# Ten gate projections of a hybrid decoder step, computed in pairs with seven block products instead of eight

## The chip, the cores and the metric

The kernel runs on one core of a Trainium2 chip. A core has five engines that run side by side and wait for one another through semaphores: TensorE (PE, matrix products; its weight loads are listed as PEld), VectorE (DVE), ScalarE (ACT), GpSimd (POOL) and SyncE (SP, which issues most DMAs). The metric is the device time of one execution in microseconds; each kernel is executed several times and the median is taken. One further execution is recorded by the hardware profiler, and all rows of the trace come from that one.

## The reference

One layer of a decoder on 512 prompt tokens and 8 sample tokens (T = 520 columns), model width 1024, all in float32:

```python
h = _rmsnorm(x, norm1_g[l]) * (1.0 + sc1) + sh1
u = h @ w_in[l]                                   # 1024 x 8192
qa, fa, ia, oga, xb, yb, ga, gb = _split_cols(u)  # eight parts of 1024 columns
... o_a = HGRN2 recurrence of qa, fa, ia, oga;  o_b = RG-LRU recurrence of xb, yb ...
merged = sigmoid(ga) * (o_a @ w_branch_a[l]) + sigmoid(gb) * (o_b @ w_branch_b[l])
x = x + g1 * (merged @ w_out[l])
h2 = _rmsnorm(x, norm2_g[l]) * (1.0 + sc2) + sh2
x = x + g2 * (square(relu(h2 @ w_ff1[l])) @ w_ff2[l])
y = _rmsnorm(x, final_norm_g)
```

The change concerns the two gate parts of `u`, `ga` and `gb`: 16 output tiles of 128 columns, each a product of a 1024 x 128 block of `w_in` with `h`.

## The kernel before, in words

Activations lie transposed: 128 features on the partitions, the 520 tokens along the free axis, in two halves of 260 (`HALF`). Every float32 operand of a large product is split into a high part (a cast to fp32r, on ACT) and a low part (the difference, on DVE). A product is then three fp32r products, high x high, high x low and low x high, summed in PSUM (`products`, L151). An output tile takes 8 blocks of the inner dimension x 3 x 2 halves = 48 products of 128 x 128 by 128 x 260 (`gemm`).

A weight tile (1024 x 128, 512 KB) is loaded by SP into one of four staging buffers (`wst`), split into `whi` and `wlo` (`_split_w`, ACT at L112, DVE at L115), and used. There are two places for split tiles in the pool `whl`; `split_place` takes them in turn (place `2 * (nsplit % 2)`), and the split of tile n + 2 is asked for when tile n is taken (`AHEAD = 2`), so it can start when the products of tile n are done.

The stages, in order: a start phase; eight HGRN2 heads taken two at a time, with the RG-LRU tiles between them; the 16 gate tiles, first eight of `gb`, then eight of `ga`; the 16 branch products (`branch` for b, `merge` for a); eight tiles of `w_out`; then the MLP, whose second product already uses seven block products for eight (`_split_pair`, `product`). The tail of the last two heads (`head_prompt` for head 6, then for head 7, then `heads_sample_done`) is a chain of small steps between PE, ACT and DVE that runs beside the gate tiles. Before the change `end_recurrences` and `begin_tail` follow gate tile b6; `begin_tail` closes the memory pools of the recurrences and calls `load_branches`, in which POOL loads the recurrences' outputs from DRAM (L885 for `o_b`, L889 for `o_a`) and ACT and DVE split them. Each gate tile is evicted by one sigmoid on ACT straight from PSUM (L175). Between the tiles lie sixteen modulation steps (`mod`, L397): each loads two row blocks of `w_mod` into `wst` and multiplies them with 16 small products into the bank `pt`.

PSUM has eight banks: two double ones (`pmm`), two of `pps`, one `ppt`, one `ppb`. The order of each engine's instructions is fixed when the program is built, by a list scheduler that follows program order as priority; `urgent()` raises an eviction's priority.

Of the kernel before, what the change touches and what calls it, by code (L numbers as in the profile page):

```python
# [35 lines left out]
ROWS = "rows"  # L36

# [6 lines left out]
BUFS = {"e": 4, "g": 6, "xb": 2, "xc": 2, "xcs": 2, "gate": 4, "ag": 2, "hs": 3, "y": 3, "ma": 8, "rs": 1, "sq": 1, "t": 5, "sqs": 2,  # L44
# [32 lines left out]
class Kernel:  # L77
# [55 lines left out]
    def ready_w(self, tile, loads=LOADS):  # L133
        while self.wnext_split < len(self.worder) and self.worder[self.wnext_split][0] <= tile:
            while self.wnext_load < min(self.wnext_split + loads, len(self.worder)):
                i = self.worder[self.wnext_load][1]
                self.wstage[i] = self._load_w(self.wspecs[i], self.wst)
                self.wnext_load += 1
            i = self.worder[self.wnext_split][1]
            st = self.wstage.pop(i)  # L140
            self.wsplit[i] = st.rearrange("p k n -> p (k n)") if ROWS in self.wspecs[i] else self._split_w(st, self.split_place())
# [52 lines left out]
    def slot(self, pool, tag, dt=F32):  # L194
        return pool.tile([128, T], dt, tag=tag, name=tag, bufs=BUFS.get(tag))

# [341 lines left out]
    def head(self, h, first=None):  # L538
# [29 lines left out]
        for j, t in enumerate((f, X[:, 1], q)):  # L568
            nc.vector.tensor_copy(fkq[:, j, :NB], t[:, L:])
# [9 lines left out]
        for b in range(NB):  # L579
            nc.scalar.activation(st[:, b], st[:, b], AF.Copy, scale=fkq[:, 0, b:b + 1])  # L580
# [17 lines left out]
    def head_sample_state(self, h, after):  # L598
        nc = self.nc
        *_, vb, st, fkq = self.opened[h]  # L600
        for b in range(NB):
            ins = nc.vector.scalar_tensor_tensor(st[:, b], vb[:, b], fkq[:, 1, b:b + 1], st[:, b], OP.mult, OP.add)
# [3 lines left out]
    def heads_sample(self, hs):  # L606
        nc = self.nc
        po = self.pps.tile([128, 512], F32, name="ps")
        for e, h in enumerate(hs):
            *_, st, fkq = self.opened[h]  # L610
            for b in range(NB):
                j, c = 32 * (b % 4), 256 * e + 128 * (b // 4)
                nc.tensor.matmul(po[j:j + 32, c:c + 128], fkq[:, 2], st[:, b], start=True, stop=True)
        return po

    def heads_sample_done(self, hs, po):
        nc = self.nc
        ev = self.hg.tile([128, 512], F32, name="sev", bufs=1)
# [7 lines left out]
    def heads_prompt(self, hs):  # L626
# [82 lines left out]
    def head_prompt(self, h, tb, at):  # L709
# [4 lines left out]
        pk = self.ppt.tile([128, 512], F32, name="pt")  # L714
# [4 lines left out]
        pkv = self.ppt.tile([128, 512], F32, name="pt")  # L719
# [10 lines left out]
        po = self.ppt.tile([128, 512], F32, name="pt")  # L730
        for c in range(NC):
            s = slice(c * C, (c + 1) * C)
            nc.tensor.matmul(po[:, s], at[:, c], vn[:, s], start=True, stop=c == 0)
            if c:
                nc.tensor.matmul(po[:, s], Q[:, s], S[:, (c - 1) * 128:c * 128], start=False, stop=True)
        o = self.slot(self.hg, "g")
        ss = self.sm.tile([128, 16], F32, name="ss")
        for c in range(NC):
            s = slice(c * C, (c + 1) * C)
            nc.scalar.activation(o[:, s], po[:, s], AF.Square, accum_out=ss[:, c:c + 1])  # L740
        nc.vector.tensor_scalar(ss[:, :NC], ss[:, :NC], 1.0 / 128, EPS, OP.mult, OP.add)
# [4 lines left out]
        pt = self.ppt.tile([128, 512], F32, name="pt")  # L746
# [1159 lines left out]
```

## Time and profile before

| | before |
|---|---|
| median of three runs | 1019.62 us (1018.96 to 1022.07) |
| the profiled execution | 1015.0 us, of which the recorded span is 1013.2 us |
| granted TensorE clock, mean | 0.995 |
| PE busy | 992.3 us, 98% of the span |
| PEld busy | 964.7 us, 95% |
| DVE busy | 673.8 us, 67% |
| ACT busy | 512.2 us, 51% |
| POOL busy | 130.4 us, 13% |
| sigmoid of the first of the eight `gb` tiles, last of them, last of the eight `ga` tiles | 396.6, 438.9 and 494.6 us |
| first product step of a branch tile a evicted | 553.3 us |

In the rows that follow, a group or an instruction names its line of the kernel, its engine, its operation and the tiles it writes and reads (`mm<-h,whi`: into PSUM tile `mm` from `h` and `whi`); then the partitions x elements of its output and input. A row of the timeline begins with the start and the duration in microseconds, `x4` means four alike merged into one row, and brackets hold the idle time before it and what ended it. A row of windows gives a stretch of the span, its length, and the busy time with the number of instructions for each engine.

### The profile page before, as it was taken

Reading aid. Unit: us, or ns where it says so; the run is one execution under the profiler, and the core shown is the slowest. Engines: PE = TensorE matmul, PEld = TensorE weight load, DVE = VectorE, ACT = ScalarE, POOL = GpSimd, SP = SyncE. Lnnn points to the kernel's source line nnn. Section 1 sums busy time; section 2 is a strip of 40 time slices with the busy share of each in tenths; the row PEclk is TensorE's granted clock in tenths of the full one; section 3 lists DMA queues with packets and bytes.
Section 4 is the critical chain, followed back from the end, with each engine's and each line's share of the span. In section 5 each row is a group of like instructions: output and inputs, shape, how many; then the busy total and the mean of one; then the engine's idle time right before and its main releaser. Section 6 shows DMA issues by size and latency. Waiting matters only on the chain. (4 is left out here: it accounts for less than half of the span.)

```text
span 1013.2 us, 23554 instructions
## 1 busy us (share of the span) xinstructions
PE 992.3 (98%) x9738; PEld 964.7 (95%) x9738; DVE 673.8 (67%) x1417; ACT 512.2 (51%) x963; POOL 130.4 (13%) x253
## 2 busy tenths in 40 slices
PE   6999999999999999999999999999999999999997
PEld 5899999999989999999999999999999999999996
DVE  7686867695785867346233448777767776777685
ACT  6364745735654573345111224466555645646663
POOL 4320000000000010002000000022321331232050
PEclk9999999999999999999999999999999999999998
DMA  9974354344344444339756787322672483273242
GB/s 298 314 214 119 97 164 127 103 122 135 107 137 116 124 147 127 95 98 304 205 167 177 231 245 207 102 86 50 151 176 64 98 196 104 53 175 86 63 84 85
DMA packets 205373, 145.80 MB, mean 144 GB/s; under 512 B 6742, under 2 KB 193774, under 8 KB 205258
## 3 DMA queue, kind: packets, MB, share of 16 engines
q1 hardware_dynamic: 194034, 128.08, 43.1%
q0 software_dynamic: 11216, 16.18, 7.4%
q8 instruction: 76, 1.25, 0.5%
q14 instruction: 31, 0.25, 0.1%
q10 hardware_dynamic: 16, 0.03, 0.0%
HBM read 123.61 MB, written 13.39 MB: 135 GB/s over the span
## 5 line engine op out<-in xcount | busy, mean ns | idle before, releaser
L151 PE MATMUL mm<-h,whi 128*128 128x260 f32 (+1 forms) x2944 | 488.5, 285 | 0.0
L151 PEld LDWEIGHTS mm<-h,whi 128*128 128x128 f32 x2944 | 409.2, 188 | 2.9 <-issue 1.4
L151 PE MATMUL mm<-h,wlo 128*128 128x260 f32 x1472 | 302.4, 285 | 0.0
L115 DVE TENSOR_TENSOR wlo<-wst,whi 128x1024 fp32r<-128x1024 f32 x164 | 200.0, 1221 | 133.5 <-ACT whi L112 132.2
L112 ACT CAST whi<-wst 128x1024 fp32r<-128x1024 f32 x164 | 171.7, 1049 | 213.6 <-PE mm L151 166.2
L151 PEld LDWEIGHTS mm<-h,wlo 128*128 128x128 f32 x1472 | 229.5, 188 | 0.9 <-issue 0.6
L151 PE MATMUL mm<-a,whi 128*128 128x260 f32 x512 | 83.0, 284 | 0.0
L151 PEld LDWEIGHTS mm<-a,whi 128*128 128x128 f32 x512 | 70.0, 188 | 2.1 <-ACT whi L112 1.6
L885 POOL DMA_DIRECT2D t<-obT_d x8 | 4.3, 541 | 396.9 <-PE pb L790 300.1
L151 PE MATMUL mm<-a,wlo 128*128 128x260 f32 x256 | 51.4, 282 | 0.0
L1262 DVE TENSOR_TENSOR f<-f 128x260 f32<-128x260 f32 x64 | 27.3, 426 | 27.8 <-ACT f L1257 27.2
L1254 POOL TENSOR_TENSOR ft<-ft,fsh 128x8 f32<-128x8 f32 x28 | 18.4, 658 | 206.6 <-DVE ft L1248 206.6
L1251 ACT ACTIVATE ft<-ft,fsh 128x512 f32<-128x512 f32 (+2 forms) x36 | 24.0, 675 | 36.0 <-DVE ft L1248 36.0
L151 PE MATMUL mm<-b,whi 128*128 128x260 f32 x256 | 41.7, 285 | 0.0
L151 PEld LDWEIGHTS mm<-a,wlo 128*128 128x128 f32 x256 | 39.4, 188 | 0.0
L151 PEld LDWEIGHTS mm<-b,whi 128*128 128x128 f32 x256 | 35.0, 188 | 2.1 <-ACT whi L112 2.1
L672 DVE TENSOR_TENSOR X<-X,tb 128x512 f32<-128x512 f32 x48 | 30.9, 684 | 5.4 <-PE ps L660 4.2
L1296 POOL DMA_DIRECT2D ma<-snap x28 | 26.5, 960 | 40.1 <-issue 32.3
L1278 POOL DMA_DIRECT2D ma<-snap x28 | 26.4, 943 | 38.0 <-DMA ma<-snap 22.7
L1257 ACT ACTIVATE f<-ft 128x520 f32<-128x520 f32 (+1 forms) x36 | 20.8, 587 | 15.0 <-POOL ft L1255 13.0
L580 ACT ACTIVATE st<-st,fkq 128x128 f32<-128x128 f32 x64 | 19.8, 395 | 14.1 <-DMA st<-in_state_hgrn_dram 12.4
L151 PE MATMUL mm<-b,wlo 128*128 128x260 f32 x128 | 25.6, 282 | 0.0
(576 smaller groups left out, 1865.5 us busy)
## 6 DMA issues: line engine op xcount, KB each, us to landing
wst<-in_w_in_dram SPq DMA_DIRECT2D x64, 512.0 KB, 4.1
wst<-in_w_mod_dram SPq DMA_DIRECT2D x32, 512.0 KB, 3.8
wst<-in_w_ff_dram SPq DMA_DIRECT2D x64, 256.0 KB, 3.6
wst<-in_w_ff_dram SPq DMA_DIRECT2D x32, 512.0 KB, 4.7
wm<-in_w_mod_dram SPq DMA_DIRECT2D x8, 1024.0 KB, 10.8
st<-in_state_hgrn_dram SPq DMA_DIRECT2D x8, 512.0 KB, 6.7
vb<-vd SPq DMA_DIRECT2D x8, 512.0 KB, 3.7
out_dram<-st SPq DMA_DIRECT2D x8, 512.0 KB, 3.9
```

Of the source, the lines that this page charges most:

```text
L112: ins = self.nc.scalar.copy(hi, st)
L115: self.nc.vector.tensor_tensor(lo, st, hi.bitcast(F32), OP.subtract)
L151: self.last_product = self.nc.tensor.matmul(ps[s][:, :c.stop - c.start], x, y[:, c], start=first and n == 0, stop=last and n == 2)
L580: nc.scalar.activation(st[:, b], st[:, b], AF.Copy, scale=fkq[:, 0, b:b + 1])
L672: last = nc.vector.tensor_tensor(half, half, factors(tbs, x, b), OP.mult)
L885: nc.gpsimd.dma_start(t, self.obT_d[n])
L1251: nc.scalar.activation(t[:, :p], t[:, :p], AF.Relu, bias=sh[:, 0:1])
L1254: eng.tensor_tensor(t[:, p:], t[:, p:], sh[:, 1:9], OP.add)
L1257: nc.scalar.activation(f, self.two(self.ft)[:, a:a + n], AF.Square)
L1262: self.nc.vector.tensor_tensor(f[:, n], f[:, a], f[:, b], op)
L1278: nc.gpsimd.dma_start(x[1][:, b], v[:, :n], accum_op=OP.add)
L1296: nc.gpsimd.dma_start(x[t][:, a], s[p], accum_op=OP.add)
```

## The change

Six tiles of `gb` (m = 0 to 5, `PLAIN`) stay as they are. The other ten (b6 and b7, then a0 to a7) are computed two at a time. A pair is a 1024 x 256 block of weights; it is seen as a 2 x 2 block matrix (even and odd blocks of the inner dimension, left and right tile), and `h` as another (even and odd blocks, two halves of the tokens). Seven block products with sums of weight blocks and sums of input blocks replace the eight plain ones; each is 4 blocks x 3 = 12 products of 260 columns.

- `begin_gates`, after tile b0, closes the recurrences' pools on the left, opens the pools `ab`, `gt`, `gw`, and calls `gate_forms`: four input sums of 128 x 4 x 260, in two halves each; eight additions of high and low part on POOL, eight sums on DVE, eight casts on ACT and eight differences on DVE. They are made once and used by all five pairs.
- `gate_load` fetches the raw weights of a pair with four DMAs of SP into the pool `gw`, which holds two pairs. `gate_split` makes one weight form after another, four products ahead (`FORMS`), in four slots (`whi` and `wlo` of the two places, each holding the high and the low part of one form). Of the four sums of weight blocks in each pair, two are on POOL (for products 5 and 7) and two on DVE (6 and 3), in place in the raw tile.
- `gate_product` issues the 12 products in a fixed order. Product 1's bank goes on to hold 1+6, 1+6+5 and so on, and is copied out between; outputs are put together by three copies and three sigmoids on ACT and three additions or subtractions on DVE for each pair.
- Eleven "marks" stand for weight tiles in the list that times the `wst` loads; they load nothing.
- `load_ob` follows product 6 of the first pair, `load_oa` the last gate product; `o_a`'s parts now lie in the memory of `h`. `end_gates` also adds one to `nsplit`.
- The last two heads' `head_prompt` run step by step side by side, head 7 in the bank `ppb`, and `heads_sample_done` stands before them. Some small tiles move (`fkq` 128 x 48, `sev` inside `X`, the rows of `rg_out` in two tiles with two DMAs for one).

```diff
-BUFS = {"e": 4, "g": 6, ...
+BUFS = {"e": 4, "g": 7, ...
@@ ready_w
-                self.wstage[i] = self._load_w(self.wspecs[i], self.wst)
+                self.wstage[i] = None if MARK in self.wspecs[i] else self._load_w(self.wspecs[i], self.wst)
...
+                self.wsplit[i] = None if st is None else self._split_w(st, self.split_place())
@@ heads_prompt
-        for e, h in enumerate(hs):
-            self.head_prompt(h, tbs[:, e], at[:, e])
-        self.heads_sample_done(hs, po)
+        last = hs[1] == H - 1
+        if last:
+            self.heads_sample_done(hs, po)
+        steps = [self.head_prompt(h, tbs[:, e], at[:, e], (self.ppb, "pb") if last and e else (self.ppt, "pt"))
+                 for e, h in enumerate(hs)]
+        for _ in zip(*steps) if last else steps[0]:
+            pass
...
-    def load_branches(self):
+    def load_ob(self):
+        self.right.close()
...
         for n in range(KO):
-            t = self.slot(self.tail, "t")
-            nc.gpsimd.dma_start(t, self.obT_d[n])
-            self.ob.append(self.split(t, self.ab, "a"))
+            t = self.slot(self.tail, "t", bufs=4)
+            self.nc.gpsimd.dma_start(t, self.obT_d[n])
+            self.ob.append(self.split(t, self.abb, "b"))
+
+    def load_oa(self):
+        nc = self.nc
+        hi, lo = (self.act.tile([128, KO, T2], F32R, tag="h", name="oa", bufs=2) for _ in range(2))
...
+    def gate_forms(self):
+        nc = self.nc
+        hi, lo = self.hs
+        self.gf = {f: ([], []) for f in (4, 5, 6, 7)}
+
+        def block(c, f):
+            e, s = divmod(f, 2)
+            t = self.slot(self.tail, "t", bufs=4).rearrange("p (k n) -> p k n", k=2)
+            x, y = (z[:, 4 * c + e:4 * c + 4:2, s * HALF:(s + 1) * HALF].bitcast(F32) for z in (hi, lo))
+            nc.gpsimd.tensor_tensor(t, x, y, OP.add)
+            return t
+
+        def done(f, t):
+            h, l = (z.rearrange("p (k n) -> p k n", k=2) for z in self.pair(self.ab, "a"))
+            nc.scalar.copy(h, t)
+            nc.vector.tensor_tensor(l, t, h.bitcast(F32), OP.subtract)
+            self.gf[f][0].append(h)
+            self.gf[f][1].append(l)
+
+        for c in range(2):
+            f1, f3 = block(c, 1), block(c, 3)
+            nc.vector.tensor_tensor(f3, f1, f3, OP.subtract)
+            done(6, f3)
+            f0 = block(c, 0)
+            nc.vector.tensor_tensor(f1, f0, f1, OP.subtract)
+            nc.vector.tensor_tensor(f0, f3, f0, OP.subtract)
+            done(5, f0)
+            done(4, f1)
+            f2 = block(c, 2)
+            nc.vector.tensor_tensor(f2, f2, f0, OP.add)
+            done(7, f2)
...
+    def gate_split(self, s):
+        nc, (i, j) = self.nc, self.gate_seq[s]
+        x11, x21, x12, x22 = self.gate_raw[i]
+        if s % FORMS == 0:
+            self.gate_hl = [f"{n}{p}" for p in (self.split_place(), self.split_place()) for n in ("whi", "wlo")]
+        for n, a, b in ((7, x11, x21), (6, x11, x22), (5, x21, x22), (3, x12, x11)):
+            if j == n:
+                (nc.gpsimd if j in (5, 7) else nc.vector).tensor_tensor(a, a, b, OP.add)
+        x = {1: x11, 7: x11, 6: x11, 2: x12, 3: x12, 5: x21, 4: x22}[j]
+        t = self.whl.tile([128, KO, 128], F32R, tag=self.gate_hl[s % FORMS], name="wgate", bufs=1)
+        hi, lo = t[:, :4], t[:, 4:]
+        nc.scalar.copy(hi, x)
+        nc.vector.tensor_tensor(lo, x, hi.bitcast(F32), OP.subtract)
+        return hi, lo
+
+    def gate_product(self, s):
+        nc, (i, j) = self.nc, self.gate_seq[s]
+        while self.gate_next < min(s + FORMS, len(self.gate_seq)):
+            n = self.gate_next
+            self.gate_banks["w", n] = self.gate_split(n)
+            self.gate_next += 1
...
+        if j == 1 or (i, j) == (0, 2):
+            banks[j] = self.pmm.tile([128, 2, 512], F32, name="mm")[:, 0]
+        elif j == 2:
+            banks[2] = self.ppb.tile([128, 512], F32, name="pb")
+        elif j == 7:
+            banks[4] = self.pps.tile([128, 512], F32, name="ps")
+        ps = banks[{7: 4, 6: 1, 5: 1, 3: 1}.get(j, j)][:, :HALF]
+        hi, lo = self.gate_banks.pop(("w", s))
+        for k in range(4):
+            for n, (x, part) in enumerate(((hi, 0), (hi, 1), (lo, 0))):
+                ins = nc.tensor.matmul(ps, x[:, k], self.gate_acts(j, part, k), start=j in (1, 7, 2) and k == n == 0,
+                                       stop=k == 3 and n == 2, skip_group_check=True)
...
+            if j in (1, 7, 6):
+                nc.scalar.copy({1: o0[:, 0], 7: o1[:, 1], 6: o1[:, 0]}[j], ps)
+            if j == (2 if i else 1):
+                nc.vector.tensor_tensor(o0[:, 0], banks[2][:, :HALF], o0[:, 0], OP.add)
+                self.sigmoid(o0[:, 0], o0[:, 0])
+            if j == 5:
+                nc.vector.tensor_tensor(o1[:, 1], o1[:, 1], ps, OP.subtract)
+            if j == 4:
+                nc.vector.tensor_tensor(o1[:, 0], ps, o1[:, 0], OP.subtract)
+            if j == (4 if i else 5):
+                self.sigmoid(o1[:, :], o1[:, :])
+            if j == 3:
+                self.sigmoid(o0[:, 1], ps)
@@ the order of the steps
+        for m in range(PLAIN):
+            one("w_in", 56 + m, lambda m: gb.update({m: self.gate(7, m, self.slot(self.ma, "ma"))}), m)
+            if m == 0:
+                steps.append(([], self.begin_gates))
+            elif m < 3:
+                steps.append(([], self.gate_load, m - 1))
+        self.gates = [("b", m) for m in range(PLAIN, KO, 2)] + [("a", m) for m in range(0, KO, 2)]
+        n, self.gate_seq = len(self.gates), []
+        for u in range(n):
+            self.gate_seq += [(u, 1), (u - 1, 3)] if u else [(0, 2), (0, 1)]
+            self.gate_seq += [(u, j) for j in ((7, 6, 2, 5, 4) if u else (7, 6, 4, 5))]
+        self.gate_seq.append((n - 1, 3))
...
+        share, due = len(mods) / (2 * n - 3 + 2 * KO), 0.0
...
+            if (u, j) == (0, 6):
+                steps.append(([], self.end_recurrences))
+                steps.append(([], self.load_ob))
+            if (u, j) == (1, 5) or u > 1 and j in (7, 5):
+                due = mod_step(due + share)
+        steps.append(([], self.end_gates))
...
+    def end_gates(self):
+        self.nsplit += 1
+        self.gws.close()
+        self.tail = self.scope.enter_context(self.tc.tile_pool(name="tail", bufs=2, reuse_waits="tile"))
+        self.load_oa()
```

More of the change, by code (lines that the diff above doesn't have):

```diff
@@ L36 @@
 ROWS = "rows"
+MARK = "mark"
+PLAIN = 6
+FORMS = 4
 NM = 9
@@ L704, in heads_prompt, with head_prompt @@
             nc.vector.tensor_copy(at[j:j + 32, :, :, j:j + 32], a32[j:j + 32])
-        for e, h in enumerate(hs):
-            self.head_prompt(h, tbs[:, e], at[:, e])
-        self.heads_sample_done(hs, po)
-    def head_prompt(self, h, tb, at):
+        last = hs[1] == H - 1
[5 more added lines that the diff above has]
+            pass
+        for _ in () if last else steps[1]:
+            pass
+        if not last:
+            self.heads_sample_done(hs, po)
+    def head_prompt(self, h, tb, at, psum):
         nc = self.nc
@@ L868, in rg_out @@
             ps = self.pps.tile([128, 512], F32, name="ps")
-            r = self.tail.tile([16, KO, 128], F32, name="rows", bufs=1)
+            r = [self.slot(self.tail, "t")[:16, :512].rearrange("p (n f) -> p n f", f=128) for _ in range(2)]
             ps2 = self.pps.tile([128, 512], F32, name="ps")
```

130 lines of the change are left out of this document (90 added, 40 removed).

## The prediction

> **What bounds the kernel now.** I read the page's busy times and slices first, then the windows around the gate tiles, then PE's timeline there.
>
> ```profile
> PE 992.3 (98%) x9738; PEld 964.7 (95%) x9738; DVE 673.8 (67%) x1417; ACT 512.2 (51%) x963; POOL 130.4 (13%) x253
> ...
> PE   6999999999999999999999999999999999999997
> ...
> POOL 4320000000000010002000000022321331232050
> ```
>
> PE is busy for 992.3 of 1013.2 us and every slice but the first and the last is full; POOL hardly works in the slices in question (16 to 20 of 40). The windows cut the stretch at the end of the eight `gb` tiles (452.4) and at the end of the `ga` tiles (500):
>
> ```profile
> 394.50:452.40 57.90, 57.65 (x596) 56.73 (x595) 23.14 (x56) 20.17 (x46) 0.00 (x0) 1.00 0.29 85
> 452.40:500.00 47.60, 47.59 (x434) 43.86 (x438) 23.51 (x49) 20.55 (x34) 6.17 (x13) 1.00 0.79 252
> 500.00:553.00 53.00, 53.00 (x476) 49.47 (x468) 17.04 (x21) 8.19 (x9) 2.10 (x4) 1.00 0.62 181
> 553.00:600.00 47.00, 47.00 (x427) 43.26 (x429) 22.27 (x31) 12.37 (x16) 3.83 (x7) 1.00 0.74 221
> ```
>
> Columns: stretch, length, then PE, PEld, DVE, ACT, POOL busy with the number of instructions, clock, DMA share, GB/s. PE idles 0.25 us in the first stretch and nothing to speak of in the others, at full clock. DVE is busy 40% to 49% and ACT 35% to 43% in the two gate stretches. So here a product of PE that goes away is time that goes away, as long as the other engines keep PE fed. What one product is worth is the pace, not the modelled 0.28 us:
>
> ```profile
> 424.74 0.65 PE L151 MATMUL mm<-h,whi 128*128 128x260 f32 x4
> ...
> 425.46 0.65 PE L151 MATMUL mm<-h,whi 128*128 128x260 f32 x4
> ...
> 426.19 0.64 PE L151 MATMUL mm<-h,whi 128*128 128x260 f32 x4
> ```
> ```profile
> 961.00:971.00 10.00, 10.00 (x84) 1.00 0.64 145
> ```
>
> From 424.74 to 425.46 to 426.19 six products each (four high, two low): 0.72 us for six, 0.120 us each. The second fence is a window of the MLP where seven-for-eight products already run back to back: 84 in 10.00 us, 0.119 us. The block form has the same pace.
>
> **What goes.** Ten gate tiles have 48 products each, 480; five pairs have 7 x 12 = 84 each, 420. Sixty products x 0.12 us = **7.2 us** off PE. Loads are the same bytes. The head tail's reordering can win at most the 0.25 us that PE idles there, and I count nothing.
>
> **What comes on ACT and DVE.** A weight tile now costs one cast and one difference:
>
> ```profile
> 437.99 1.05 ACT L112 CAST whi<-wst 128x1024 fp32r<-128x1024 f32 x1 [5.03 <-PE mm L151]
> 438.94 0.60 ACT L175 ACTIVATE ma<-mm 128x520 f32<-128x520 f32 x1
> ```
> ```profile
> 387.39 1.28 DVE L672 TENSOR_TENSOR X<-X,tb 128x512 f32<-128x512 f32 x2
> ...
> 439.07 1.23 DVE L115 TENSOR_TENSOR wlo<-wst,whi 128x1024 fp32r<-128x1024 f32 x1 [1.19 <-ACT whi L112]
> ```
>
> The cast of 1024 columns starts when PE has finished the tile before last, takes 1.05 us, then 1.23 us on DVE; a sigmoid 0.60. (387.39 shows two DVE operations of 512 columns in a row: 1.28 us, 0.64 each.) After the change the forms have 512 columns and evictions 260; their rows, from the MLP and the recurrences:
>
> ```profile
> L175 ACT ACTIVATE gate<-pb,pa 128x260 f32<-128x260 f32 x32 | 15.3, 480 | 11.8 <-PE pb L790 11.8
> ...
> L1106 ACT CAST xhi<-wst 128x512 fp32r<-128x512 f32 x16 | 9.6, 621 | 0.7 <-DMA wst<-in_w_ff_dram 0.7
> ...
> L1181 ACT ACTIVATE snap<-ps,modT 128x260 f32<-128x260 f32 x15 | 7.2, 477 | 1.3 <-PE ps L1159 0.9
> ```
> ```profile
> L1118 DVE TENSOR_TENSOR wst<-wst 128x512 f32<-128x512 f32 x16 | 10.9, 682 | 0.1
> ...
> L1109 DVE TENSOR_TENSOR xlo<-wst,xhi 128x512 fp32r<-128x512 f32 x16 | 10.7, 686 | 1.0 <-ACT xhi L1106 1.0
> ...
> L1290 DVE SCALAR_TENSOR_TENSOR ma<-pt,modT,ma 128x260 f32<-128x260 f32 x14 | 6.8, 482 | 1.5 <-PE pt L1159 1.5
> ...
> L206 DVE TENSOR_TENSOR a<-t,a 128x520 fp32r<-128x520 f32 x8 | 5.4, 690 | 1.3 <-ACT a L205 1.3
> ```
>
> Per pair on ACT: seven casts (0.62), three copies (0.48), sigmoids of 260, 260 and 520 (0.48 + 0.48 + 0.60): 7.3 us. On DVE: seven differences and two weight sums (9 x 0.64 = 5.8 us) and three evictions (0.48): 7.2 us. PE takes 84 x 0.12 = 10.1 us for the pair. Both engines fit below PE, ACT well (73%), DVE closely (71%), and there is more on DVE:
>
> ```profile
> 454.36 0.22 DVE L761 TENSOR_SCALAR sq<-ps 128x64 f32<-128x64 f32 x1
> ...
> 462.52 0.22 DVE L764 TENSOR_TENSOR os<-os,ogs 128x64 f32<-128x64 f32 x1
> ```
>
> `end_recurrences` is a string of fifteen small DVE operations from 454.36 to 462.52 (about 0.22 us each, 3.3 us), and `load_ob` brings eight differences of 520 columns (8 x 0.645 = 5.2 us, the L206 row less the overlap seen at 387.39). Both now fall into the first pairs. DVE over the five pairs: 36.0 + 3.3 + 5.2 = 44.5 us. PE over the same: 50.4 us and about five modulation steps (seven due points x 16/23) at 1.07 us:
>
> ```profile
> 506.51 1.07 PE L397 MATMUL pt<-wst,cT 128*32 128x256 f32 x16
> 507.51 0.61 PE L873 MATMUL ps<-ident,xlast 128*11 128x128 f32 x4
> ```
>
> 55.7 us in all. So DVE has 11.2 us to spare, if nothing else holds it up. The 16 x 0.645 = 10.3 us that `gate_forms` puts on DVE (half as much on ACT) lie beside b1 to b5, where DVE idles 34.8 us of 57.9; with its eight POOL additions (9.6 us, below) it is some 20 us of about 36, together with the head tail's own work. Hidden; were that cover gone, product 7 of the first pair would wait, which I price below.
>
> **GpSimd's additions.** No POOL addition of 512 columns is in the trace. The nearest rows:
>
> ```profile
> L1838 POOL MEMSET at<- 128x1024 f32 x1 | 1.0, 965 | 0.0
> ...
> L233 POOL IOTA tc<- 128x520 int32 x1 | 0.6, 557 | 0.0
> ```
> ```profile
> 49.02 0.56 POOL L69 TENSOR_TENSOR fs<-fs,shp 128x64 f32<-128x64 f32 x1
> ```
>
> Writing 520 columns takes 0.56 us, writing 1024 takes 0.97 (0.94 ns a column), adding 64 columns 0.56. The lower end is 0.56 us. The upper end takes the step from an unhindered addition of 8 columns (0.19, below) to that 0.56 as if it were all size: 6.6 ns a column, 3.5 us for 512. It is not all size:
>
> ```profile
> 48.71 0.69 DVE L69 TENSOR_TENSOR h<-ht,h 128x512 fp32r<-128x512 f32 x1 [0.26 <-ACT h L69]
> ```
> ```profile
> 660.96 1.04 POOL L1254 TENSOR_TENSOR ft<-ft,fsh 128x8 f32<-128x8 f32 x1 [58.76 <-DVE ft L1248]
> ...
> 662.65 0.19 POOL L1254 TENSOR_TENSOR ft<-ft,fsh 128x8 f32<-128x8 f32 x1
> ```
> ```profile
> 660.73 1.22 DVE L115 TENSOR_TENSOR wlo<-wst,whi 128x1024 fp32r<-128x1024 f32 x1
> ```
>
> At 48.71 DVE begins a difference that ends at 49.40; the POOL addition begun at 49.02 ends 0.18 later. At 660.96 a POOL addition of 8 columns lasts 1.04 us and ends at 662.00, when the DVE difference begun at 660.73 has just ended; the same instruction at 662.65 takes 0.19. A POOL addition does not run while a DVE difference of two SBUF operands runs. I therefore stand near the memset row: two inputs read one after the other at 0.94 ns x 512 each plus 0.2, **1.2 us**. The Trainium skill (SBUF — State Buffer, "Who interferes with whom") says why and goes further: a DVE instruction with two SBUF inputs and a GpSimd instruction that reads SBUF share a read port, and whoever starts first blocks the other wholly. The trace agrees for POOL (1.04 against 0.19 us); that DVE waits for POOL no row can show, since these additions are too short. The Trainium skill also gives the addition about 2.6 cycles a column at 1.2 GHz (GPSIMD Engine Reference, "Elementwise — side-by-side cycle accounting"), an estimate of 1.1 us here.
>
> The rows show one side of the lock; I take it that it holds for both. Ten additions (two for each pair) then take 12.0 us of DVE's 11.2 spare: 0.8 us too much, on PE's path. Were DVE not held, that 0.8 would be nothing; at the lower end too.
>
> **Latency.** A form's slot is free when the product four before it is done, so cast, difference and sum have three products, 4.3 us. Cast 0.62 and difference 0.69 with two hand-overs are 1.5 us, a sum ahead of them up to 1.9 (1.2 and a DVE operation awaited). Form 6 hangs on 7, and 7 on 1, in place in the same raw block: 1.5 + (1.9 + 1.5) + (0.7 + 1.5) = 7.1 us from the start of form 1, which may start 4.3 us before product 1; product 6 starts 4.3 us after it (1, 3 and 7 come first): 8.6 us, 1.5 spare. Hence no stall in the quiet pairs. In pairs 0 and 1, bursts of `o_b` differences (four land together, 2.6 us) and POOL's queue, where eight DMA issues stand among the additions and wait for free `t` buffers, eat that spare. I take **1.2 us** of stalls; the ends are 0 and 4 (twice 2.6 less 1.5, and 2 for forms that come late at product 7).
>
> Evictions between the uses of a bank have 1.4 to 2.9 us (one or two products) for 0.48: nothing.
>
> **Loads.** A pair is four DMAs, asked for at product 1 of the pair before, when pair u - 2's buffers are free, and needed about five products later, 7.2 us:
>
> ```profile
> wst<-in_w_in_dram SPq DMA_DIRECT2D x64, 512.0 KB, 4.1
> ...
> wst<-in_w_ff_dram SPq DMA_DIRECT2D x64, 256.0 KB, 3.6
> ...
> t<-obT_d POOLq DMA_DIRECT2D x8, 260.0 KB, 5.4
> ```
>
> A 512 KB tile lands in 4.1 us, 256 KB in 3.6, a tile of `o_b` in 5.4. The stretch moves about 12 MB (three pairs 3.1, `o_b` 2.1, five modulation steps of 1.05, three branch tiles 1.6) in 55.7 us, 215 GB/s; 252 was reached from 452.4 on. Hidden, with little room.
>
> **The way out.** `gate_hl` calls `split_place` twice for every four slots, nine times, 18 calls; branch tile b0 is the 19th, b1 the 20th, then `end_gates` adds one, so b2 is the 22nd and has b1's place. b2's cast can only start when b1's products end: 1.05 + 1.23, less the four products that need only the high part (0.48), 1.8 us. Against that, `rg_out`'s 16 transposes (4 in 0.61) stand just before b2 and a modulation step (1.07) may, 3.5 us of other PE work, if the order puts it there. I take half, **0.9 us**; ends 0 and 1.8. `load_oa` needs `h` free and lies beside eight b branch tiles of 5.8 us, where DVE is 32% busy: hidden. `shifts` now waits for the last branch product, which `out_proj` waits for anyway.
>
> **The sum.** -7.2 + 0.8 + 1.2 + 0.9 = **-4.3 us**: the profiled execution of 1015.0 us would become 1010.7. The median of the three runs, 1019.62, lies 4.6 above it; I forecast on its scale: 1015.3 us. By the Trainium skill's 1.1 us for an addition the sum would be -7.2 + 0 + 1.2 + 0.9 = -5.1, 1014.5.
>
> **Rivals.** *Slower: GpSimd's lock makes DVE the bound.* Place: the five pairs. Spare is 11.2 us for ten additions; beyond 1.12 us each, every 0.1 us costs 1.0 us of PE. With the other terms (2.1) it decides where an addition holds DVE (7.2 - 2.1 + 11.2) / 10 = 1.63 us. At 2.4, the middle between my value and the upper end, it is 24.0 - 11.2 = 12.8 of stalls, -7.2 + 12.8 + 2.1 = +7.7: 1027.3 us; at the upper end +18.7. For it: the 1.04 us row, and that the only POOL additions seen are of 64 columns or less. Against: evictions read PSUM and 0.18 us remain of the 64-column addition once DVE lets go. The Trainium skill speaks for this case (GPSIMD Engine Reference, "Engine selection": elementwise belongs on VectorE, GpSimd is about twice as slow): twice the 0.64 us of the row at 387.39 is 1.28, short of the deciding 1.63.
>
> *Everything is hidden:* the slack holds and POOL work lies where DVE idles: -7.2, 1012.4 us.
>
> *The gain is spent on waiting at fixed points:* a pair's load shares the queues with as much of `o_b` or `w_mod` (2.1 MB at 252 GB/s is 8.3 us, 1.1 late for each of three pairs, 3.3), and b2 pays its full 1.8: -7.2 + 0.8 + 1.2 + 3.3 + 1.8 = -0.1, 1019.5 us. For it: 215 of 252 GB/s; against: `w_in` tiles that land in 4.1 us now.
>
> **How the numbers follow.** Forecast (-2 to -6.2, centre -4.3) 0.50, all hidden 0.20, spent on waits 0.12, slower 0.18. 0.3% (3.1 us) is about what a measurement tells here, so faster means below 1016.6: all of "hidden" and 0.41 of the forecast, 0.61; same: 0.09 of the forecast and 0.11 of the waits, 0.20; slower the rest, 0.19. The likeliest case has 1013.4 to 1017.6 of its own. The range runs from the hidden case less 1.9 for scatter between runs to halfway into the slower one: 1010.5 to 1024.
>
> **What would show it.** Right: 60 fewer PE products; POOL additions of 512 columns at 1.0 to 1.5 us; DVE above 85% busy between the first and last pair; PE idle or stretched by 2 to 4 us in all, in pairs 0 and 1 and around b2. Wrong: additions over 1.6 us, DVE differences that last longer while POOL adds, PE waiting on `wgate`; or waits at `gw` loads.

## The result, and the profile after

The changed kernel took 1028.27 us (median of 4 runs, 1025.25 to 1030.2) against 1019.29 us of the kernel before in the same comparison: ratio 1.0091, 95% interval 1.0062 to 1.0120. It is slower by 9 us; I had forecast 4.3 us faster. The profiled execution took 1030.2 us, with a span of 1028.4.

The page's busy times:

```profile
PE 997.7 (97%) x9678; PEld 964.6 (94%) x9678; DVE 718.0 (70%) x1483; ACT 530.9 (52%) x1016; POOL 161.5 (16%) x275
```

The 60 products are gone (9738 to 9678), and yet PE is busy 5.4 us longer. The columns of windows are as in the prediction. First the kernel before, from the last sigmoid into `X` (the end of the last head's projections) to the first product of `out_proj`, and from there to the end; then the same for the kernel after, with the first stretch also cut at the first and behind the last product of the pairs:

```profile
351.94:600.82 248.88, 246.92 (x2504) 233.41 (x2502) 119.19 (x236) 85.31 (x148) 14.79 (x29) 1.00 0.57 175
600.82:1013.20 412.38, 405.67 (x3352) 404.56 (x3348) 297.75 (x516) 231.71 (x424) 89.50 (x151) 0.99 0.46 114
```
```profile
355.59:615.02 259.43, 246.76 (x2443) 228.24 (x2442) 166.66 (x307) 105.19 (x203) 45.96 (x51) 0.99 0.57 176
355.59:435.83 80.24, 74.96 (x961) 72.80 (x960) 64.17 (x127) 39.41 (x81) 19.75 (x14) 1.00 0.42 125
435.83:507.61 71.78, 65.08 (x536) 57.04 (x535) 50.52 (x110) 38.51 (x87) 16.43 (x17) 0.95 0.54 173
...
615.02:1028.40 413.38, 407.19 (x3352) 405.95 (x3348) 294.54 (x511) 230.58 (x423) 89.31 (x151) 0.99 0.44 109
```

The stretch that the change touches grew from 248.9 to 259.4 us, 10.5 us; PE idles in it 12.7 us, before 2.0. The rest grew by 1.0. The remaining 3.7 us lie ahead of the stretch (it begins at 355.6 and not 351.9). Part of that belongs to this one execution: in a second profile of the same kernel (e0, below) the stretch begins at 353.9; it lasts 258.8 there.

What PE waits for, in the kernel after (us in all, times, longest):

```profile
PE pt L403 <- DMA wst<-in_w_mod_dram: 7.0, 5, 5.4
PE ps L666 <- DVE X L682: 3.4, 4, 1.0
...
PE ps L670 <- DVE X L678: 2.8, 1, 2.8
```

The second row stands in the kernel before too (3.3 us at its line 660). New are 2.8 us for a difference of the heads' tail (`X`, line 678) and 7.0 us for rows of `w_mod`. The first of these in DVE's timeline, and what POOL does at that time:

```profile
395.07 3.53 DVE L678 TENSOR_TENSOR X<-X,tb 128x512 f32<-128x512 f32 x2
...
402.57 1.28 DVE L678 TENSOR_TENSOR X<-X,tb 128x512 f32<-128x512 f32 x2
...
410.02 3.48 DVE L678 TENSOR_TENSOR X<-X,tb 128x512 f32<-128x512 f32 x2
```
```profile
394.15 7.33 POOL L938 TENSOR_TENSOR t<-h 128x520 f32<-128x520 f32 x4 [333.88 <-ACT ma L181]
404.94 2.16 POOL L938 TENSOR_TENSOR t<-h 128x520 f32<-128x520 f32 x1 [3.46 <-DVE t L954]
409.63 3.31 POOL L938 TENSOR_TENSOR t<-h 128x520 f32<-128x520 f32 x2 [2.53 <-DVE a L944]
```
```profile
413.55 1.15 PE L670 MATMUL ps<-X 128*64 128x64 f32 x16 [2.85 <-DVE X L678]
```

Two `X` differences take 1.28 us at 402.57, when POOL is idle, and 3.53 and 3.48 us at 395.07 and 410.02, when POOL adds. So the lock that one side of the prediction's rows showed holds for both: DVE waits for POOL as POOL waits for DVE. (The Trainium skill, SBUF — State Buffer, "Who interferes with whom", says that a VectorE instruction with two SBUF inputs contends with a GpSimd instruction that reads SBUF, and that the order of issue decides which of them is blocked. The trace agrees that VectorE can be the one: 3.5 against 1.28 us.) PE stands for 2.85 us behind the pair at 410.02. DVE's busy time counts the standing still besides the forms' own work, and in those stretches it is full where before it had two thirds free; the kernel before, then after:

```profile
400.00:410.00 10.00, 10.00 (x114) 9.59 (x114) 3.71 (x5) 4.03 (x7) 0.00 (x0) 1.00 0.33 97
410.00:420.00 10.00, 10.00 (x87) 10.00 (x86) 2.58 (x6) 2.74 (x11) 0.00 (x0) 1.00 0.20 59
```
```profile
400.00:410.00 10.00, 10.00 (x111) 9.82 (x110) 9.82 (x15) 4.95 (x9) 4.01 (x3) 1.00 0.77 211
410.00:420.00 10.00, 6.87 (x86) 6.16 (x86) 9.90 (x11) 2.69 (x5) 5.17 (x3) 1.00 0.17 54
```

The long wait for `w_mod`, in PE's timeline, and the windows around it:

```profile
469.84 1.08 PE L403 MATMUL pt<-wst,cT 128*32 128x256 f32 x8 [5.45 <-DMA wst<-in_w_mod_dram]
470.85 2.97 PE L1022 MATMUL mm<-h,wgate 128*128 128x260 f32 x12
473.61 0.57 PE L1022 MATMUL ps<-a,wgate 128*128 128x260 f32 x2
```
```profile
463.00:470.00 7.00, 1.55 (x16) 1.37 (x18) 6.01 (x10) 3.59 (x7) 1.71 (x2) 0.80 0.90 312
470.00:474.00 4.00, 4.00 (x22) 3.13 (x17) 0.00 (x0) 0.15 (x1) 0.00 (x0) 0.50 0.46 135
474.00:476.00 2.00, 2.00 (x21) 1.48 (x20) 1.23 (x2) 1.27 (x3) 0.00 (x0) 1.00 0.19 37
```

PE idles for 5.45 us and is then granted half the clock: twelve products take 2.76 us (470.85 to 473.61) in place of the 1.44 of twelve at the prediction's pace. That makes the wait some 2 us dearer than it looks (4.0 us at a clock of 0.50).

### The profile page after: what moved, and what is told of

Read it like the earlier page. It is cut to its first block, busy times and chain, and to the rows that moved or that the text cites. A ratio compares the mean times of both kernels' runs of the same rounds, so it can differ in the third digit from the quotient of the medians.

```text
span 1028.4 us, 23634 instructions
## 1 busy us (share of the span) xinstructions
PE 997.7 (97%) x9678; PEld 964.6 (94%) x9678; DVE 718.0 (70%) x1483; ACT 530.9 (52%) x1016; POOL 161.5 (16%) x275
## 5 line engine op out<-in xcount | busy, mean ns | idle before, releaser
L157 PE MATMUL mm<-h,whi 128*128 128x260 f32 x2624 | 435.9, 285 | 0.0
L157 PEld LDWEIGHTS mm<-h,whi 128*128 128x128 f32 x2624 | 365.4, 189 | 1.1 <-issue 0.2
L157 PE MATMUL mm<-h,wlo 128*128 128x260 f32 (+1 forms) x1312 | 270.7, 285 | 0.0
L157 PEld LDWEIGHTS mm<-h,wlo 128*128 128x128 f32 x1312 | 204.9, 188 | 1.0 <-issue 0.6
L157 PE MATMUL mm<-oa,whi 128*128 128x260 f32 x256 | 41.9, 285 | 0.0
L157 PE MATMUL mm<-a,whi 128*128 128x260 f32 x256 | 41.3, 283 | 0.0
L996 DVE TENSOR_TENSOR wgate<-gw,wgate 128x512 fp32r<-128x512 f32 x35 | 28.7, 825 | 15.5 <-ACT wgate L995 9.5
L157 PEld LDWEIGHTS mm<-oa,whi 128*128 128x128 f32 x256 | 34.9, 188 | 2.5 <-issue 0.8
L157 PEld LDWEIGHTS mm<-a,whi 128*128 128x128 f32 x256 | 35.1, 188 | 0.4 <-issue 0.4
L403 PE MATMUL pt<-wst,cT 128*32 128x256 f32 x256 | 21.1, 395 | 7.0 <-DMA wst<-in_w_mod_dram 7.0
```

The lines of the kernel that those rows point to most:

```text
L157: self.last_product = self.nc.tensor.matmul(ps[s][:, :c.stop - c.start], x, y[:, c], start=first and n == 0, stop=last and n == 2)
L403: self.nc.tensor.matmul(ps[32 * j:32 * j + 32, :256], self.cT[:, k, :], w[:, 256 * j:256 * j + 256], start=k == 0, stop=k == KO - 1)
L996: nc.vector.tensor_tensor(lo, x, hi.bitcast(F32), OP.subtract)
```

## The experiments

Each ratio is to the kernel before, run on the same chip. My theory after the profile: GpSimd's lock holds VectorE, and what is late there makes PE wait. The rival: the rows of `w_mod`, which the list scheduler places among the products of the pairs, come late by themselves.

**e0: the changed kernel again; e1: all additions on VectorE; e2 and e3: the modulation products kept behind the preceding gate product.**

```diff
# e1: gate_forms and gate_split
-            nc.gpsimd.tensor_tensor(t, x, y, OP.add)
+            nc.vector.tensor_tensor(t, x, y, OP.add)
-                (nc.gpsimd if j in (5, 7) else nc.vector).tensor_tensor(a, a, b, OP.add)
+                nc.vector.tensor_tensor(a, a, b, OP.add)
# e2: mod_rows, while the pairs run (e3: both edits)
+            if self.in_gates:
+                self.behind(ins, self.last_product)
```

> The changed kernel as it is, once more. Three losses stand in its first trace beside the 7.2 us won: (A) PE waits 6.3 us for rows of w_mod between 455 and 470 us and then works at half the granted clock for some 3 us more (about 9.5 us in all); (B) GpSimd's additions hold DVE, and PE waits 2.9 + 0.4 us for X in the last heads' tail; (C) the start phase ends 3.8 us later, at half clock after a wait of 0.6 us for wm. If A and B belong to the program and C to the execution, A and B come back within a microsecond or two and C may not; if all three are the program's, the end of the start phase is again near 58.6 us against 54.7 before. Ratio to before 1.007 to 1.011 either way.

> All additions of GpSimd (eight for the input forms, ten weight sums) on VectorE instead, nothing else. If the lock (B) is the main cause, the time falls by 6 us or more, DVE's 512-column differences go back to 0.69 us at most, and the waits for X near 398 and 413 us go. If the late rows of w_mod (A) are the main cause, the waits for w_mod stay and the time falls by 2 to 4 us only; a DVE too full for its work would instead show up as PE waiting for weight forms, and the time would rise.

> The w_mod products of the gate stage are kept behind the gate product that stands before them in the program; before, the scheduler had pulled several of them ahead on PE. Nothing else is changed; GpSimd keeps its additions. If A is the main cause, PE's waits for w_mod (6.3 us) and the half clock behind them go and the time falls by 8 to 10 us, to about that of the kernel before or 1 us under it. If the lock is the main cause, the time falls by less than 3 us and PE waits for weight forms in the places that are left.

> Both edits at once. If A and B are separate and add up, about 12 us less than the changed kernel: 3 us under the kernel before (ratio about 0.997), with PE idle under 4 us from the last heads to the end of the gates. If they hide one another, no better than the better one of the two.

Measured: e0 1.0086 (1.0060 to 1.0113), e1 0.9986 (0.9969 to 1.0004), e2 1.0060 (1.0038 to 1.0082), e3 1.0011 (0.9986 to 1.0036). Moving the additions off GpSimd gives back 10 us, although VectorE has more work by it. In e1 the stretch lasts 246.75 us, 2.1 less than before the change. VectorE is as full between 400 and 410 us as in the kernel after, but its `X` differences are not held up; the wait for `X` at line 678 is gone, and the waits for `w_mod` shrink without having been touched:

```profile
353.10:599.85 246.75, 242.20 (x2444) 226.41 (x2442) 163.49 (x325) 106.25 (x204) 16.76 (x33) 1.00 0.61 185
353.10:429.27 76.17, 74.48 (x962) 72.77 (x960) 62.71 (x136) 39.60 (x78) 2.17 (x4) 1.00 0.45 132
429.27:492.33 63.06, 60.99 (x537) 55.22 (x535) 48.84 (x120) 38.42 (x88) 4.81 (x9) 1.00 0.62 197
```
```profile
PE pt L403 <- DMA wst<-in_w_mod_dram: 1.9, 4, 0.9
```

Against the kernel after, 4.1 us come back ahead of the pairs (80.24 to 76.17) and 8.7 us in them (71.78 to 63.06). In e2 the wait for `w_mod` fell to 1.4 us, but PE now waits for evictions of gate products, which it did not before, on ACT (3.2 us) more than on VectorE (1.3 us). The longest, 2.1 us, is for an ACT copy that stands behind the cast of an `o_b` tile, for which ACT had waited 2.54 us:

```profile
PE mm L1025 <- ACT gp L1036: 3.2, 2, 2.1
```

The late rows are thus for the most part a symptom: moving the additions gives back four times what pinning does (0.0100 against 0.0026), and once they are on VectorE, pinning wins nothing more (e3).

**e4 and e5: which additions? e6: the lock without the result. e7: the order of the last heads.** e4 is the first half of e1's edit, e5 the second. e6 is e1 and besides it ten GpSimd additions whose results nobody uses; e7 is e1 with `last = False` in `heads_prompt`.

```diff
# e6, at the end of gate_split
+        for _ in range(2 if j == 5 else 0):
+            nc.gpsimd.tensor_tensor(x21, hi.bitcast(F32), hi.bitcast(F32), OP.add)
```

> The changed kernel with the eight additions of the input forms on VectorE and the ten weight sums left on GpSimd. With all eighteen on VectorE it took 1016.6 us, with all on GpSimd 1026.8. Theory A (each group costs by the time for which it holds VectorE: eight forms of 1.76 us are 14.1 us, ten sums of 1.30 are 13.0): about half of the 10 us comes back, 1021 to 1023; the 2 to 2.9 us wait of PE for X in the last heads' tail is gone, the waits for w_mod rows among the gate products stay at 2 us or more. Theory B (the forms do it all: the backlog that they leave on VectorE at the end of the heads' tail is what makes the pairs late): 1016 to 1018. Theory C (the sums do it all): 1025 to 1027.

> The complement: the ten weight sums on VectorE, the eight additions of the input forms left on GpSimd. Theory A: 1020 to 1023, with the wait of PE for X of 2 to 2.9 us still there and the waits for w_mod rows below 2 us. Theory B: 1024 to 1027. Theory C: 1016 to 1018.

> All eighteen additions on VectorE as in the 1016.6 us kernel, and besides them ten additions of 512 columns on GpSimd, two for each pair once its form 5 is cast, written into a raw block that is read no more: nobody waits for their results. Theory lock (what costs is that VectorE stands still while GpSimd adds): ten times 1.3 us more on a VectorE with some 4 us to spare in the pairs, 1020 to 1026, with wgate differences of up to 1.8 us in the trace. Rival (what costs is that the weight forms wait for GpSimd's results, which come late): no difference from 1016.6, 1015.5 to 1018.

> All eighteen additions on VectorE, and the last two heads in the old order: head 6, then head 7, both in the bank pt, heads_sample_done behind them. My prediction counted nothing for that part: 1015.6 to 1017.6. Rival (side by side the two tails fill each other's waits while VectorE is busy with the forms): slower by 2 to 5 us, 1018.5 to 1021.5, with PE waiting in the tail between 400 and 435 us.

Measured: e4 0.9983 (0.9963 to 1.0003), e5 1.0047 (1.0017 to 1.0076), e6 0.9967 (0.9942 to 0.9993), e7 1.0080 (1.0053 to 1.0107). The time of e4, 1017.89 us, lies in theory B: with the eight input forms on VectorE the ten sums may stay on GpSimd for nothing, although they hold VectorE up visibly. The time of e5, 1023.73 us, lies just below B's range and just above A's: with the forms left on GpSimd, moving the sums may win some of the 10 us after all (1.0047 against 1.0086, with intervals that overlap). So the forms are the main cause, and the sums may cost something only beside them. The `wgate` differences of e4, then of e1 (us in all, mean ns of one):

```profile
L996 DVE TENSOR_TENSOR wgate<-gw,wgate 128x512 fp32r<-128x512 f32 x35 | 28.4, 821 | 9.0 <-ACT wgate L995 8.6
```
```profile
L996 DVE TENSOR_TENSOR wgate<-gw,wgate 128x512 fp32r<-128x512 f32 x35 | 23.7, 688 | 11.7 <-ACT wgate L995 11.4
```

4.7 us more on VectorE, and no time lost: in the pairs it has that to spare. e6 says the same and refutes what I had written for the lock there: 1015.91 us, where I expected 1020 to 1026, with VectorE busy for 87% of the pairs. e7 surprised me: the old order of the last heads beside the pairs costs 9.6 us. PE's timeline there shows where; the products of the plain tiles have run out, and the tail's own chain is in the open:

```profile
441.89 0.81 PE L749 MATMUL pt<-g,at 128*128 128x128 f32 x4 [2.01 <-DVE g L741]
...
449.71 1.11 PE L768 MATMUL pt<-ident,g 128*128 128x128 f32 x4 [4.86 <-ACT g L763]
```

**e8 and e9: four pairs. e10: the lock alone in the tail. e11: the heads' order alone.** e8 is e4 with `PLAIN = 8` (and `end_recurrences`, `load_ob` after tile b6); e9 has the same and the forms on GpSimd. e11 is the kernel before with the changed `heads_prompt`, `head_prompt` and `heads_sample_done`.

```diff
# e10: e1, and in gate_forms, done()
+            nc.gpsimd.tensor_tensor(junk, x, h.bitcast(F32), OP.add)   # x: a block of hi
# and in the order of the steps
-            elif m < 3:
-                steps.append(([], self.gate_load, m - 1))
+            elif m in (2, 5):
+                steps.append(([], self.gate_load, m // 5))
```

> Input forms on VectorE, weight sums on GpSimd (0.998 of before with ten tiles in pairs), but with all eight gb tiles left plain and only the eight ga tiles in pairs: 48 products fewer than before instead of 60, and two more plain tiles, 11.5 us of PE work, for VectorE to catch up behind the forms and the heads' tail; end_recurrences and the o_b loads come after the seventh plain tile. Theory backlog (the forms crowd VectorE at the tail, what they leave is paid in the first pairs): 0.992 to 0.996 of before, the 1.4 us of lost saving more than won back, no PE wait for w_mod over 1 us in the pairs. Rival (every pair pays its own way, in waits and switching): a smaller saving in proportion, 0.997 to 1.000.

> The same with the input forms on GpSimd, as in the changed kernel (1.0086 of before). Theory backlog: the additions still hold VectorE in the heads' tail and PE still waits there for X (2 to 3 us), but two more plain tiles take up what is left: 0.996 to 1.002. Rival (every pair pays): 1.005 to 1.008.

> All eighteen additions on VectorE (0.9986 of before), and besides them eight additions of 520 columns on GpSimd, one behind the cast of each input form, into a weight buffer that is not yet loaded (the second pair's load is asked for at tile b5 instead of b2); nobody waits for their results. Theory lock (VectorE stands still while GpSimd adds, in the tail where it has nothing to spare): X differences of 1.0 us mean instead of 0.69, a PE wait for X or for the pairs' forms, 1.003 to 1.010. Rival (what costs in the changed kernel is that the forms wait for GpSimd one after another, 1.8 to 2.2 us each): 0.997 to 1.000.

> The kernel before with nothing but the new order of the last two heads (side by side, heads_sample_done ahead of them). My prediction counted at most 0.25 us for it: 0.998 to 1.002. Rival (the order is worth by itself the 12 us that its removal cost beside the pairs): 0.988 to 0.994.

Measured: e8 0.9976 (0.9954 to 0.9998), e9 1.0036 (1.0008 to 1.0064), e10 1.0029 (1.0005 to 1.0054), e11 1.0006 (0.9980 to 1.0032). e8 lies in its rival's range (every pair pays its own way) and not in the backlog theory's. e10 is the cleanest evidence for the lock: eight additions that nobody waits for, in that place, cost 0.0043 over e1, some 4 us. The sign that I had named, `X` differences of 1.0 us, was wrong: they kept their 0.69 us (two take 1.28 at 413.90). POOL held other operations that stand ahead of them in VectorE's order, and so they came late. The rows of POOL, of VectorE and of PE:

```profile
404.81 5.03 POOL L947 TENSOR_TENSOR gw<-h,a 128x520 f32<-128x520 f32 x3 [4.94 <-ACT a L943]
```
```profile
406.87 1.80 DVE L938 TENSOR_TENSOR t<-h 128x520 f32<-128x520 f32 x1
...
413.90 1.28 DVE L678 TENSOR_TENSOR X<-X,tb 128x512 f32<-128x512 f32 x2
```
```profile
415.24 0.66 PE L730 MATMUL pb<-ident,X 128*128 128x128 f32 x4 [1.65 <-DVE X L678]
...
430.87 1.23 PE L749 MATMUL pt<-g,at 128*128 128x128 f32 x4 [2.06 <-DVE g L741]
```

PE's two waits are 3.7 us together; e1 has neither. The second pair is loaded later than in e1, so part of e10's 3.1 us of waits for `w_mod` (e1: 1.9) may be that. e9 lies between the ranges of the two theories, and its trace parts the loss in two: the two more plain tiles take up what the forms leave to the pairs (0.3 us of waits for `w_mod`, 7.0 in the kernel after), but the wait in the tail itself stays:

```profile
PE ps L670 <- DVE X L678: 2.8, 1, 2.8
...
PE pt L403 <- DMA wst<-in_w_mod_dram: 0.3, 1, 0.3
```

e11 is what the prediction said: by itself the heads' order is worth nothing.

**e12 to e15: what became of the saving.** e12 is e1 with no modulation step asked for among the pairs, e13 the same with `PLAIN = 8`, e14 is e1 without the extra step of `nsplit`, e15 is e14 with `PLAIN = 8`.

```diff
# e12, e13: the order of the steps
-        share, due = len(mods) / (2 * n - 3 + 2 * KO), 0.0
+        share, due = len(mods) / (2 * KO), 0.0
-            if (u, j) == (1, 5) or u > 1 and j in (7, 5):
-                due = mod_step(due + share)
# e14, e15: end_gates
-        self.nsplit += 1
```

> All eighteen additions on VectorE (0.9986 of before), and the program asks for no modulation step among the pairs: the sixteen steps go one behind each of the sixteen branch tiles. Theory rows (the steps among the pairs cost the missing gain: their rows land late, each step breaks a product group): the waits for w_mod in the pairs below 0.5 us, 0.993 to 0.997. Rival (VectorE sets the pace of the pairs: about 51 us of work for it against 50 us of products, and the steps only gave it time): waits move to wgate and evictions, 0.997 to 1.001.

> Four pairs instead of five (eight plain gb tiles), all additions on VectorE, and the modulation steps behind the branch tiles only. Theory rows: 0.993 to 0.997, as with five pairs. Rival: VectorE has two plain tiles, 11.5 us, to catch up, but in the pairs it is again the one that is waited for: 0.996 to 0.999.

> All eighteen additions on VectorE, without the extra step of nsplit in end_gates, so that branch tile b2 has the other place. My prediction priced the place conflict at 0.9 us, with 0 and 1.8 as ends. If b2 is covered by other PE work already: 0.997 to 1.000, as with it. If it costs what I said: lower by 0.001 to 0.002; and a tile further on may pay for it instead.

> Four pairs instead of five, all additions on VectorE, no extra step of nsplit, the modulation steps where the changed kernel has them. If a pair saves nothing on balance (with the input forms on VectorE, five pairs gave 0.9983 and four 0.9976): 0.997 to 0.999. If each pair pays its own way: 0.9985 to 1.0005. If the pairs' backlog was what ate the gain: 0.993 to 0.996.

Measured: e12 0.9999 (0.9967 to 1.0031), e13 0.9998 (0.9978 to 1.0018), e14 0.9988 (0.9964 to 1.0012), e15 1.0000 (0.9983 to 1.0018). All four lie within 0.0012 of 1, e13 above both of its ranges. e12 and e13 do less than they ask for: the list scheduler still places two of the sixteen modulation steps among the pairs (32 of their products, 96 in e1), and one of them waits 2.0 us for its rows. With four steps fewer there nothing is won; in e12 PE waits for weight forms instead (2.4 us). What pairs without any such step would take is not tested. b2 costs nothing (e14 against e1). No placing that I tried is clearly faster than the kernel before; the best, e6 and e8, have intervals that end just below 1, and are two of fifteen variants.

## Why the prediction was wrong, point by point

**The step that failed** is "Hidden", said of `gate_forms` "beside b1 to b5, where DVE idles 34.8 us of 57.9; with its eight POOL additions (9.6 us, below) it is some 20 us of about 36". Three things were wrong in it. The additions were too cheap: 15.0 us for eight, not 9.6,

```profile
L938 POOL TENSOR_TENSOR t<-h 128x520 f32<-128x520 f32 x8 | 15.0, 1897 | 341.1 <-ACT ma L181 333.9 <-DVE a L944 3.8 <-DVE t L954 3.5
L991 POOL TENSOR_TENSOR gw<-gw 128x512 f32<-128x512 f32 x10 | 14.2, 1423 | 41.0 <-DVE wgate L996 40.6
```

for additions of a kind, two inputs of 520 columns, that I had no row for (the shortest of the eight took 1.62 us). The idle time was taken from too long a stretch. The 57.9 us run on beyond b7 to the first `ga` tile (452.4; the last `gb` tile is evicted at 438.9, and 396.6, given above for the first, is b1). In the kernel before b1 to b5 last from 389.7 to 426.2:

```profile
389.70:426.20 36.50, 36.50 (x476) 35.56 (x475) 17.11 (x38) 12.41 (x27) 0.00 (x0) 1.00 0.31 91
```

VectorE idles there for 19.4 us and not 34.8. The forms' 10.3 us and the lock's 9.6 would have filled that even at my price; at 15.0 they are 25.3 and don't fit. In e1, with the additions on VectorE itself (5.3 us), they are 15.6 and do. And I asked only for room: the additions fall between 394.2 and 416.4, beside the `X` differences of the last heads' tail, a chain on which PE waits, and each one that meets them holds them up. What I named as the price, product 7 of the first pair, did not wait; the tail did (2.8 us), and the `w_mod` rows behind it came late. The forms on GpSimd are worth about 0.006 to 0.010 of the kernel's time (e5 against e1, after against e4).

**-7.2 us** for 60 products: the count was right, the pace nearly. In e1 PE is busy 4.7 us less over the stretch than before (246.92 to 242.20) and idles 2.6 us more (1.96 to 4.55), so that 2.1 us are left of the 7.2. Of the difference between 7.2 and 4.7 a part is seen in e1's timeline: modulation steps are cut into eights, and each change of kind costs.

```profile
447.31 0.64 PE L403 MATMUL pt<-wst,cT 128*32 128x256 f32 x8
447.88 1.70 PE L1022 MATMUL mm<-a,wgate 128*128 128x260 f32 x12
449.41 1.60 PE L1022 MATMUL pb<-h,wgate 128*128 128x260 f32 x12
450.95 1.07 PE L403 MATMUL pt<-wst,cT 128*32 128x256 f32 x16
451.95 1.33 PE L1022 MATMUL mm<-a,wgate 128*128 128x260 f32 x9
```

Eight take 0.57 us and sixteen 1.00, twice eight 0.14 more; twelve products behind a modulation step and twelve ahead of one take 1.53 and 1.54 (447.88, 449.41) in place of 1.44. Added up over PE's rows of the stretch, from start to start without the idle times, products are 6.2 us less in e1 than before, modulation steps 1.2 us and the rest 0.2 us more.

**+0.8 us** for VectorE over-full in the pairs: there were no such stalls. Additions of 1.42 us mean stand above my 1.2 and within the range that I had called right for the pairs, but VectorE was busy 50.5 of 71.8 us there, 70%, not the 85% that I gave as the sign; e4 and e6 show that with the forms on VectorE the lock is free in the pairs.

**+1.2 us** of latency: in the kernel after no wait of PE for `wgate` stands among its rows. The term was nothing in this place; in e12 such waits exist (2.4 us).

**+0.9 us** at b2: nothing. `rg_out`'s last eight transposes and half a modulation step stand right ahead of its first product at 521.07, as the cover that the prediction named:

```profile
519.53 1.03 PE L893 MATMUL ps<-ident,hlast 128*9 128x128 f32 x8
520.50 0.64 PE L403 MATMUL pt<-wst,cT 128*32 128x256 f32 x8
```

**Loads "hidden, with little room"**: wrong by the 7.0 us of waits for `w_mod` and the half clock behind the longest. That they follow the lateness of VectorE is shown by e1, which didn't touch them; the path from the one to the other (the stores of the heads' tail stand in SP's queue among these loads; four `o_b` tiles wait for VectorE to free `t`) I have only argued from the order of the queues. That the DMA engines were simply full (0.90 of their time between 463 and 470 us, 312 GB/s, above) can have a part in it; no run separates the two.

**The heads' order, "I count nothing"**: right alone (e11), wrong as a part: without it the pairs lose 10 us more (e7). I take it that the change removes two of the plain tiles under which the old order was hidden; the forms' work on VectorE beside the tail would be another reason, and no run separates them.

**The rivals.** The slower one had the right cause and sign, and its 1027.3 us is near the measured time, but by accident: its place, the five pairs, was wrong. At the 1.42 us that an addition took, its rule (1.0 us of PE for each 0.1 us beyond 1.12) would give 3.0 us of stalls in the pairs, and e4 shows no wait for `wgate`. "Wrong" was to be told by "DVE differences that last longer while POOL adds"; they did, on `wgate` too (825 ns a piece, 688 in e1), but it cost time where they stood in the tail.

What stays open: how the 2.6 us of added idle time in e1 would go away, and why one pair fewer (e15) and five (e1, e14) come out alike within 0.002.

## What to carry to other kernels

Before work is moved to GpSimd, look for what VectorE has to do in that same stretch: VectorE stands still beside an addition there, and here that was free only where VectorE had time left and no chain that PE waits for ran through it. Take the idle time from the very stretch in which the new work will stand; then ask which chain runs there and what each of its links will meet. A reordering that is worth nothing alone can be what makes another part of the change bearable, so test parts by taking them away as well as by adding them.

## What was not expected of the hardware

PE can pay for an idle time a second time, at half the clock. Behind 5.45 us PE was granted half the clock for about 4 us (470 to 474, above) and then all of it; behind the 2.85 us at 413.55 the clock stayed at 1.00 (410 to 420, above). The Trainium skill (TensorE: Matmul & The Clock Gate, "Part 1: The HAM clock gate") puts the border at an idle window of about 3.4 us, and these two rows agree. Other runs here don't: in e9 the same wait for `X`, again 2.85 us and up to 415.4, was followed by 3.4 us at half the clock, and in e5 one of 1.86 us by as much. So the length of the wait alone doesn't decide:

```profile
415.40:418.80 3.40, 3.37 (x44) 3.16 (x48) 3.40 (x3) 0.00 (x0) 2.20 (x1) 0.51 0.20 39
```

What I can't place is the start phase of the profile after, with a clock of 0.52 for 11 us, PE busy in the records throughout:

```profile
23.00:34.00 11.00, 11.00 (x59) 9.40 (x60) 4.03 (x9) 1.71 (x3) 0.63 (x3) 0.52 1.07 362
```

An addition on GpSimd that begins ahead of VectorE's instruction isn't seen to be slowed by it: 1.04 us for 512 columns in e6 (both operands the same tile), the shortest of its ten. VectorE, which begins 0.04 us later, pays alone: 1.57 us where the same difference takes 0.69 without POOL. Nor does VectorE always win by beginning first in the trace: at 452.01 it begins 0.34 us ahead of an addition that takes 1.05 us, and its difference takes 1.97.

```profile
449.88 1.04 POOL L998 TENSOR_TENSOR gw<-wgate 128x512 f32<-128x512 f32 x1 [9.40 <-DVE wgate L996]
```
```profile
449.92 1.57 DVE L212 TENSOR_TENSOR b<-t,b 128x520 fp32r<-128x520 f32 x1
...
452.01 1.97 DVE L212 TENSOR_TENSOR b<-t,b 128x520 fp32r<-128x520 f32 x1
...
454.88 0.69 DVE L212 TENSOR_TENSOR b<-t,b 128x520 fp32r<-128x520 f32 x1
```
